# A hybrid S5 and dilated-attention layer: the turns of q and k stand apart, and V is two tiles

## The chip, the cores and the metric

The kernel runs on one core of a Trainium2 chip. A core has five engines, each with an instruction queue of its own that it works off in order: TensorE (PE; its weight loads are shown as PEld), VectorE (DVE), ScalarE (ACT), GpSimd (POOL) and SyncE (SP), which here mostly issues DMAs. [...] The metric is the time of one execution on the device in microseconds, the median of the runs.

## The reference

One decoder layer of width 1024 over 512 tokens, batch 1, everything in float32. A root-mean-square norm is followed by one wide projection, whose columns feed an S5 branch (a complex state-space scan with gates), an attention branch with a gate, and two merge gates. The branches are projected, gated, added, projected once more and added to the input. The attention branch is what the change touches:

```python
DILATED_GROUPS = ((128, 1), (512, 4), (2048, 16))
...
        h = rms_norm(x, norm_w[layer])
        proj = h @ w_in[layer].astype(f32)
        u_s, z_s, q, k, v, z_a, r_s, r_a = jnp.split(proj, offsets, axis=-1)
        y_s = s5_branch(u_s, ...)
        y_s = (y_s * jax.nn.silu(z_s)) @ w_ssm_out[layer].astype(f32)
...
        y_a = dilated_attention(q, k, v)      # q, k normed and rotated
        y_a = (y_a * jax.nn.silu(z_a)) @ w_attn_out[layer].astype(f32)
        m = jax.nn.sigmoid(r_s) * y_s + jax.nn.sigmoid(r_a) * y_a
        x = (x.astype(f32) + m @ w_o[layer].astype(f32)).astype(x.dtype)
...
        for g, (window, dil) in enumerate(DILATED_GROUPS):
            j = jnp.arange(window // dil + 1)
            idx = t[:, None] - dil * j[None, :]
            s = jnp.einsum('bqhd,bqjhd->bqhj', q_blk[:, :, g], kg) * scale
            lse = jax.nn.logsumexp(s, axis=-1)
            p = jnp.exp(s - lse[..., None])
            outs.append(jnp.einsum('bqhj,bqjhd->bqhd', p, vg))
            lses.append(lse)
        w = jax.nn.softmax(jnp.stack(lses), axis=0)
        return jnp.einsum('gbqh,gbqhd->bqhd', w, jnp.stack(outs))
```

Each of the 8 heads (64 wide) has three groups of q, k and v. Group 0 has dilation 1 and needs, for a block of 128 queries, its own block of keys and the one before it. Groups 1 and 2 are the dilated ones.

## The kernel before, in words

**Precision.** Every projection is done in three matmuls (`mm3`, L122): a number is split into a high part that TensorE can multiply at full speed and the rest, and hi·hi, hi·lo and lo·hi are added in PSUM. A weight tile arrives raw by DMA (`w_raw`, two buffers), ACT rounds it (`w_hi`, L108) and DVE or POOL subtracts (`w_lo`, L110); of these two there are three buffers each.

**Stages.** The program first does norm, S5 branch and gates; from about 440 us on it does the attention for four pairs of heads (loop `for hp in range(NP)`, L1094 to L1120), and then the last projections. In the loop for the pair `hp`:

- `scores(hp)`: products of queries and keys (tile `sps`), softmax on ACT, DVE and POOL. The result is `Pt`, the probabilities of both heads and both kinds: kind 0 is group 0, kind 1 the two dilated groups.
- `qk_first()`: a wide granule of projections (tile `pj`, four banks) that gives q and k of groups 0 and 1 for the next pair; norm on DVE, rotation on POOL (L852 to L857). The rotated results are the tiles `qraw`.
- `qk_second(hp + 1, mid)`: the granule that gives q and k of group 2 (`qraw`, copied by L903, their squares by L879 and L882) and V of groups 1 and 2 (copied by L905). It goes through the contraction in four steps `kq`, each with four rows of tokens `r`, and calls `mid` once per `kq`. `mid` puts in, between the projections: for kq = 1 the turn of group 0, for kq = 2 the turn of group 1, for kq = 3 the values of this pair.
- `v0_unit(hp + 1, V)`: the projection of V of group 0, then the turn of group 2, then `finv()`, which writes V of group 0 (L593).

A **turn** (`qk_turn`, L859) transposes q, and then k, of one group: four transposes into one PSUM bank (tile `qtp`, L67), from which ACT writes the high part (L873) and DVE the low part (L874). For k of groups 1 and 2 these are two halves of 64 partitions.

The **values** (`values`, L987) go in four pieces: kind 0 in two halves, then kind 1 in two halves. A piece transposes the probabilities of each head (four transposes into one bank, tile `ptp`; the first of kind 0 has three), ACT copies the bank of the first head to SBUF (`ptb`, L1027) and DVE that of the second (L1029); then TensorE multiplies with V (tile `ot`, L63, 30 products in all in one bank). The products of a piece stand behind the transposes of the next one. At the end DVE takes `ot` with its gate (L1036) and the result is split into `aT`.

**Banks.** `qtp`, `ptp`, `sps` and `vtp` share three banks (`ps_g`), `pj` has four (`ps_p`), and `ot` one (`ps_o`).

**V** is one tile for all three groups (`new_v`, L601, tag s6a, a single buffer). So every copy into it for the next pair waits for the last product that reads it for this one.

**What sets the order.** The code is written in the order above, but a scheduler of the framework orders the instructions of each engine by its own model of durations before the kernel is compiled. `with queued():` (L69) holds what stands under it behind the last matmul issued so far. On the chip an engine then works off its list in that order, and waits at each instruction for what it needs. In the names below, `pj<-hT_hi,w_hi` means output `pj` from inputs `hT_hi` and `w_hi`.

Of the kernel before, what the change touches and what calls it, by code (L numbers as in the profile page):

```python
# [11 lines left out]
F32 = mybir.dt.float32  # L12
# [8 lines left out]
P = 128  # L21
# [31 lines left out]
def tile_hybrid_block(ctx: ExitStack, tc: tile.TileContext, x, positions, norm_w, w_in, lam_re, lam_im,  # L53
# [529 lines left out]

    def v0_unit(hp, V):
        ps = cm_unit(hT_hi, hT_lo)
        vt = t2k("vt")
        act.copy(vt.rearrange("p (b r j) -> p r b j", r=4, b=4), ps.rearrange("p (r b j) -> p r b j", r=4, b=4))

        def finish():
            pt = bank("vtp")  # L590
            for b in range(NB):
                pe.transpose(pt[:, b * P:(b + 1) * P], vt[:, b * P:(b + 1) * P], ident)
            act.copy(V[:, 0].rearrange("p b c -> p (b c)"), pt)  # L593
        return finish

    def v_granule(hp, V):
        pss = tok_granule()
        for b in range(2):
            act.copy(V[:, 1:3, 2 * b:2 * b + 2], pss[b].rearrange("p (r g c) -> p g r c", r=2, g=2))

    def new_v():  # L601
        return big.tile([P, NG, NB, P], F32, name="V", tag="s6a")

# [213 lines left out]
    def wide_granule(th, tl, mid=None):  # L817

        pss = [ps_p.tile([P, 512], F32, name="pj", tag="pj") for _ in range(NB)]
        for kq in range(4):  # L820
            if mid:
                mid(kq)
            hi, lo = get_w()
            for r in range(NB):
                for k in range(2):
                    kk = 2 * kq + k
# [31 lines left out]

    def qk_turn(g, raw, QT, KA, KB):  # L859
        for a in range(2):  # L860
            ps = bank("qtp")
# [4 lines left out]
            if a == 0 or g == 0:  # L866
                parts = [(slice(0, P), QT[0][:, g], QT[1][:, g]) if a == 0 else (slice(0, P), KA[0], KA[1])]
            else:
                parts = [(slice(64 * h, 64 * h + 64), KB[0][64 * h:64 * h + 64, g - 1, h],
                          KB[1][64 * h:64 * h + 64, g - 1, h]) for h in range(2)]  # L870
            for sl, hi, lo in parts:
                w = wcol[sl, g, a:a + 1]
# [23 lines left out]
    def qk_second(hp, mid=None):  # L896
# [5 lines left out]
        for r in range(NB):  # L902
            act.copy(raw[:, r], pss[r][:, 0:256])  # L903
            squares(sq[:, r], pss[r][:, 0:256])
            act.copy(V[:, 1:3, r], pss[r][:, 256:512].rearrange("p (g c) -> p g c", g=2))  # L905
        qk_norm((2,), [raw], sq)
# [81 lines left out]
    def values(hp, Pt, V):  # L988
# [4 lines left out]
        def pv(kind, bb, pts):  # L993
            for i in range(2):
                b = 2 * bb + i
                for k in range(2):
                    if kind == 0 and b == 0 and k == 0:
                        continue
                    for h in range(2):
                        po = slice(64 * h, 64 * h + 64)  # L1000
                        if kind == 0:
                            v = V[:, 0, b - 1 + k, po]
                            o = ov[po, b]
                        else:
                            v = V[:, 1 + k, b, po]
                            o = ot[po, b * P:(b + 1) * P]
                        first = kind == 0 and b == 0
                        pe.matmul(o, v, pts[h][:, (2 * i + k) * P:(2 * i + k + 1) * P], start=first,
                                  stop=kind == 1 and b == NB - 1 and k == 1, skip_group_check=True)

        n = 0
        for kind in range(2):
            for bb in range(2):
# [80 lines left out]
    for hp in range(NP):  # L1094
        Pt = scores(hp, *QK)
        if hp < NP - 1:
            raws = qk_first()

            def mid(kq):
                if kq == 1:  # L1100
                    qk_turn(0, raws[0], *QK)
                if kq == 2:
                    with queued():
                        qk_turn(1, raws[1], *QK)
                if kq == 3:
                    values(hp, Pt, V)

            raw, V_next = qk_second(hp + 1, mid)
            V = V_next
            finv = v0_unit(hp + 1, V)  # L1110
            qk_turn(2, raw, *QK)
            finv()
        else:
# [3 lines left out]
            for c in range(n_ra + 1, KT - 2):  # L1117
                ra_unit(c)
            values(hp, Pt, V)
            for c in range(KT - 2, KT):  # L1120
# [61 lines left out]
```

## Time and profile before

| | |
|---|---|
| runs of the kernel before | 732.35, 732.63 and 736.42 us |
| median of them | 732.63 us |
| span of the profiled execution | 732.57 us |
| TensorE busy | 699.6 us (95%) |
| VectorE, ScalarE, GpSimd busy | 457.1, 314.6, 191.7 us |
| TensorE busy in the stretch of the four pairs (440 to 670 us) | 224.0 of 230.0 us |
| DMA, over the span | 82.14 MB, 112 GB/s |

A row of the timeline has the start in us from the span's start, the duration, engine, line and operation, output and inputs, the tile's size, how many instructions are put together in it, and in brackets the idle time of the engine before it with what it waited for. A matmul's row shows the time until its result is there, and the next one starts earlier than that, so the distance between the starts of two rows tells what a row takes on the engine.

### The profile page before, as it was taken

The page shows a single profiled execution, that of the slowest core. Times are in us where ns is not written, and L with a number is a line of the kernel's source. Part 1 is how long each engine was busy: PE and PEld are TensorE (multiplying, and loading weights), DVE is VectorE, ACT ScalarE, POOL GpSimd, SP SyncE. Part 2 cuts the span into 40 slices and gives each one's busy share as a digit, 9 for nine tenths or more (in the row PEclk, how much of TensorE's full clock was granted, in tenths as well). Part 3 has the DMA queues.
Part 4 walks back from the last instruction along what each step waited for, and adds up shares of the span by engine and source line. Part 5 has one row for each costly group of instructions (what it writes and reads, how often), then busy time and mean ns, then how long its engine had stood idle before and what let it go on. Part 6 is the DMA issues. An engine that isn't in the chain of part 4 may idle for free.

```text
span 732.6 us, 12680 instructions
## 1 busy us (share of the span) xinstructions
PE 699.6 (95%) x4821; PEld 574.2 (78%) x4821; DVE 457.1 (62%) x912; ACT 314.6 (43%) x631; POOL 191.7 (26%) x346
## 2 busy tenths in 40 slices
PE   2799899999999999999999999999989999999997
PEld 2687688778878787888888888788868877878886
DVE  6759673989946546764335659655664666464832
ACT  6434463332326465442144456537153734443420
POOL 3426540230205343550000316021601250230000
PEclk9999999999999999999999999999999999999999
DMA  8433653564547554455333432222412231326441
GB/s 203 106 96 94 171 144 77 137 149 132 120 131 153 122 103 133 139 168 172 99 100 87 130 87 79 66 58 58 115 31 79 65 89 30 115 73 236 139 144 57
DMA packets 137213, 82.14 MB, mean 112 GB/s; under 512 B 32696, under 2 KB 125632, under 8 KB 137024
## 3 DMA queue, kind: packets, MB, share of 16 engines
q1 hardware_dynamic: 135088, 78.96, 37.5%
q0 software_dynamic: 2048, 2.36, 2.6%
q8 instruction: 38, 0.62, 0.4%
q14 instruction: 23, 0.19, 0.1%
q10 hardware_dynamic: 16, 0.00, 0.0%
HBM read 68.46 MB, written 10.49 MB: 108 GB/s over the span
## 4 chain that ended last, share of the span: by engine, by line
PE 87%; DMA 4%; ACT 3%; DVE 3%; SPq 2%; issue 1%; ACTq 0%
PE pj L63 71%; DMA w_raw<-in_w_in_dram 3%; PE sps L63 3%; PE yps L63 3%; PE ot L63 2%; PE ptp L67 2%; PE kps L63 2%; PE xps L63 1%; PE qtp L67 1%; DMA Uj<-ud 1%; ACT w_hi L108 1%; SPq L442 1%; PE wps L67 1%; ACT qkp L873 1%; DVE w_lo L110 1%
## 5 line engine op out<-in xcount | busy, mean ns | idle before, releaser
L108 ACT ACTIVATE w_hi<-w_raw 128x1024 fp32r<-128x1024 f32 x100 | 106.0, 1061 | 236.8 <-PE pj L63 206.6
L110 DVE TENSOR_TENSOR w_lo<-w_raw,w_hi 128x1024 fp32r<-128x1024 f32 x98 | 124.3, 1268 | 107.9 <-ACT w_hi L108 107.2
L63 PE MATMUL pj<-hT_lo,w_hi 128*128 128x512 f32 (+1 forms) x344 | 132.9, 387 | 3.0 <-DVE hT_lo L251 3.0
L63 PE MATMUL pj<-hT_hi,w_hi 128*128 128x512 f32 (+1 forms) x344 | 132.8, 389 | 2.4 <-ACT V L905 1.4
L63 PE MATMUL pj<-hT_hi,w_lo 128*128 128x512 f32 (+1 forms) x344 | 132.4, 386 | 1.6 <-DVE w_lo L110 1.6
L63 PE MATMUL pj<-w_hi,hT_hi 128*128 128x512 f32 (+1 forms) x288 | 106.5, 372 | 0.0
L63 PE MATMUL pj<-w_lo,hT_hi 128*128 128x512 f32 (+1 forms) x288 | 106.5, 370 | 0.0
L63 PE MATMUL pj<-w_hi,hT_lo 128*128 128x512 f32 (+1 forms) x288 | 106.0, 371 | 0.0
L63 PEld LDWEIGHTS pj<-hT_lo,w_hi 128*128 128x128 f32 x344 | 66.0, 192 | 16.2 <-DVE hT_lo L251 3.9
L63 PEld LDWEIGHTS pj<-hT_hi,w_hi 128*128 128x128 f32 x344 | 65.5, 192 | 16.5 <-ACT V L905 2.1
L63 PEld LDWEIGHTS pj<-hT_hi,w_lo 128*128 128x128 f32 x344 | 65.9, 192 | 15.4 <-DVE w_lo L110 2.3
L63 PEld LDWEIGHTS pj<-w_hi,hT_hi 128*128 128x128 f32 x288 | 54.1, 188 | 10.0 <-issue 0.2
L63 PEld LDWEIGHTS pj<-w_hi,hT_lo 128*128 128x128 f32 x288 | 54.0, 188 | 10.0
L63 PEld LDWEIGHTS pj<-w_lo,hT_hi 128*128 128x128 f32 x288 | 54.0, 188 | 9.8
L931 ACT ACTIVATE Pt<-Pt,st 128x256 f32<-128x256 f32 (+1 forms) x64 | 31.0, 492 | 18.7 <-DVE st L929 18.7
L735 POOL TENSOR_TENSOR kt<-kt,dg 16x128 f32<-16x128 f32 x8 | 4.6, 571 | 125.0 <-ACT kt L734 118.4
L852 POOL TENSOR_TENSOR rt<-qraw,tC 128x256 f32<-128x256 f32 x12 | 14.3, 1189 | 87.7 <-DVE qraw L846 87.4
L739 POOL DMA_DIRECT2D dd<-kt x64 | 33.7, 535 | 2.4 <-POOL kt L735 2.4
L874 DVE SCALAR_TENSOR_TENSOR qkp<-qtp,wcol,qkp 128x512 fp32r<-128x512 f32 (+1 forms) x32 | 23.0, 745 | 13.5 <-ACT qkp L873 13.4
L961 POOL COPY sw<-st 32x4 f32<-32x4 f32 x64 | 12.0, 187 | 73.2 <-ACT Pt L931 70.5
L873 ACT ACTIVATE qkp<-qtp,wcol 128x512 fp32r<-128x512 f32 (+1 forms) x32 | 20.8, 685 | 15.7 <-PE qtp L67 10.4
L277 POOL TENSOR_TENSOR ab<-dd,AT 128x512 f32<-128x512 f32 x16 | 23.0, 1446 | 11.6 <-DVE ab L278 11.6
(263 smaller groups left out, 1289.4 us busy)
## 6 DMA issues: line engine op xcount, KB each, us to landing
w_raw<-in_w_in_dram SPq DMA_DIRECT2D x40, 512.0 KB
w_raw<-in_w_in_dram SPq DMA_DIRECT2D x112, 128.0 KB
w_raw<-in_w_glu_dram SPq DMA_DIRECT2D x8, 512.0 KB
w_raw<-in_w_ssm_out_dram SPq DMA_DIRECT2D x8, 512.0 KB
w_raw<-in_w_o_dram SPq DMA_DIRECT2D x8, 512.0 KB
x_all<-in_x_dram SPq DMA_DIRECT2D x4, 512.0 KB
ud<-uT SPq DMA_DIRECT2D x8, 256.0 KB
Uj<-ud SPq DMA_DIRECT2D x8, 256.0 KB
```

The costliest lines, as they stand in the source:

```text
L63: last[0] = nc.tensor.matmul(*a, **k)
L67: last[0] = nc.tensor.transpose(*a, **k)
L108: act.activation(hi, src, AF.Copy, scale=scale)
L110: e.tensor_tensor(lo, src, hi.bitcast(F32), op=ALU.subtract)
L277: eng.tensor_tensor(tv, a2.unsqueeze(2).broadcast_to(sh), ai, op=ALU.mult)
L442: sp.dma_start(D1[64 * h:64 * h + 64, a], bv[a][h])
L739: pool.dma_start(M[Q * t:Q * t + Q, :, 0:P - Q * t], kt[:, :, t:].rearrange("q g k p -> q g (k p)"))
L852: pool.tensor_tensor(t1, rh[:, :, :, 0:16], cv.broadcast_to([P, NB * 2, 2, 16]), op=ALU.mult)
L873: act.activation(hi, ps[sl], AF.Copy, scale=w)
L874: dve.scalar_tensor_tensor(lo, ps[sl], w, hi.bitcast(F32), op0=ALU.mult, op1=ALU.subtract)
L931: act.activation(o, o, AF.Exp, bias=nm, scale=-1.0, accum_out=st[:, kind, 1, h, b:b + 1])
L961: pool.tensor_copy(sw[32 * r:32 * r + 32, :, :, b], st[32 * b:32 * b + 32, 1, :, :, r])
```

## The change

- **V is two tiles.** `V0` (group 0, tag s6c) and `V` (groups 1 and 2, tag s6a). The copies L593 and L905 write to the one or the other.
- **The values come in two parts, the dilated groups first.** `values` is now a generator: kind 1, then a pause, then kind 0. The flags `start` and `stop` of the accumulation in `ot` are set accordingly. The first part is called from `mid` at (kq, r) = (3, 2), the second behind the whole granule, both held behind the last matmul. In the last loop both parts run one after the other.
- **A turn is put in by halves.** `qk_turn` takes the list of its parts (0 is q, 1 is k), and `mid` is called before each block of rows `r`: q of group 0 at (2, 1), k of group 0 at (2, 2), q of group 1 at (3, 0), k of group 1 at (3, 1), all held behind the last matmul.

```diff
@@ finish, v_granule, new_v
-            act.copy(V[:, 0].rearrange("p b c -> p (b c)"), pt)
+            act.copy(V[0].rearrange("p b c -> p (b c)"), pt)
...
-        return big.tile([P, NG, NB, P], F32, name="V", tag="s6a")
+        return (big.tile([P, NB, P], F32, name="V0", tag="s6c"), big.tile([P, 2, NB, P], F32, name="V", tag="s6a"))
@@ the granule that calls mid
         for kq in range(4):
-            if mid:
-                mid(kq)
             hi, lo = get_w()
             for r in range(NB):
+                if mid:
+                    mid(kq, r)
@@ qk_turn
-    def qk_turn(g, raw, QT, KA, KB):
-        for a in range(2):
+    def qk_turn(g, raw, QT, KA, KB, parts=(0, 1)):
+        for a in parts:
@@ qk_second
-            act.copy(V[:, 1:3, r], pss[r][:, 256:512].rearrange("p (g c) -> p g c", g=2))
+            act.copy(V[1][:, :, r], pss[r][:, 256:512].rearrange("p (g c) -> p g c", g=2))
@@ values
-                            v = V[:, 0, b - 1 + k, po]
+                            v = V[0][:, b - 1 + k, po]
...
-                            v = V[:, 1 + k, b, po]
+                            v = V[1][:, k, b, po]
...
-                        first = kind == 0 and b == 0
+                        first = kind == 1 and b == 0 and k == 0
...
-                                  stop=kind == 1 and b == NB - 1 and k == 1, skip_group_check=True)
+                                  stop=kind == 0 and b == NB - 1 and k == 1, skip_group_check=True)
...
-        for kind in range(2):
+        for kind in (1, 0):
+            if kind == 0:
+                yield
@@ the loop over the pairs
-            def mid(kq):
-                if kq == 1:
-                    qk_turn(0, raws[0], *QK)
-                if kq == 2:
+            done = values(hp, Pt, V)
+            steps = {(2, 1): (0, 0), (2, 2): (0, 1), (3, 0): (1, 0), (3, 1): (1, 1)}
+
+            def mid(kq, r):
+                if (kq, r) in steps:
+                    g, a = steps[kq, r]
                     with queued():
-                        qk_turn(1, raws[1], *QK)
-                if kq == 3:
-                    values(hp, Pt, V)
+                        qk_turn(g, raws[g], *QK, parts=(a,))
+                if (kq, r) == (3, 2):
+                    with queued():
+                        next(done)

             raw, V_next = qk_second(hp + 1, mid)
+            with queued():
+                next(done, None)
...
-            values(hp, Pt, V)
+            for _ in values(hp, Pt, V):
+                pass
```

What the scheduler makes of it is seen in the engines' lists. A row there is line, operation, output and inputs, shape, and the number of equal instructions in a row. The first 1747 rows of TensorE are the same in both kernels.

On TensorE in the second loop (hp = 1), from the end of the granule's projections on, the list of before is:

```order
L67 MATMUL qtp<-ident,qraw 128x4x32 x8
L67 MATMUL qtp<-ident,qraw 128x128 x8
L67 MATMUL ptp<-ident,Pt 128x128 x10
L63 MATMUL ot<-ptb,V 64x4x32
L67 MATMUL ptp<-ident,Pt 128x128 x4
L63 MATMUL ot<-ptb,V 64x4x32 x5
L67 MATMUL ptp<-ident,Pt 128x128 x4
L63 MATMUL ot<-ptb,V 64x4x32
L67 MATMUL ptp<-ident,Pt 128x128 x4
L63 MATMUL ot<-ptb,V 64x4x32 x7
L67 MATMUL ptp<-ident,Pt 128x128 x8
L63 MATMUL ot<-ptb,V 64x128 x16
```

And at the same place after the change (products of shape 64x128 are the dilated groups, 64x4x32 group 0):

```order
L67 MATMUL qtp<-ident,qraw 128x4x32 x8
L67 MATMUL qtp<-ident,qraw 128x128 x8
L67 MATMUL ptp<-ident,Pt 128x128 x12
L63 MATMUL ot<-ptb,V 64x128
L67 MATMUL ptp<-ident,Pt 128x128 x4
L63 MATMUL ot<-ptb,V 64x128 x7
L67 MATMUL ptp<-ident,Pt 128x128 x3
L63 MATMUL ot<-ptb,V 64x128
L67 MATMUL ptp<-ident,Pt 128x128 x3
L63 MATMUL ot<-ptb,V 64x128 x7
L67 MATMUL ptp<-ident,Pt 128x128 x8
```

The sixteen turns' transposes stay where they were. The dilated products come first; behind the last row shown stand six products of group 0, and the other eight follow between the next granule's projections, one behind 19 of them and seven behind three more. In the third loop the list is the same but for these eight, which stand together, and in before but for the two middle pieces, which stand as x8 and x8. In the first loop the four turns of after stand apart between projections, the products form seven runs (1, 7, 1, 7, 1, 5 and 8) where there were four (1, 5, 8 and 16); in the last loop there are four runs (8, 1, 7, 14) where there were three (6, 8, 16).

On ACT in the second loop, before, from the first turns' high parts (`qkp`) to the copies of V:

```order
L873 ACTIVATE qkp<-qtp,wcol 128x512 x2
L903 COPY qraw<-pj 128x256 x4
L873 ACTIVATE qkp<-qtp,wcol 128x512
L873 ACTIVATE qkp<-qtp,wcol 64x512
L1027 COPY ptb<-ptp 128x384
L873 ACTIVATE qkp<-qtp,wcol 64x512
L1027 COPY ptb<-ptp 128x512 x3
L879 ACTIVATE qsq<-pj 128x256
L905 COPY V<-pj 128x2x128
```

After (the copy of `ptb` is L1029 there):

```order
L903 COPY qraw<-pj 128x256
L879 ACTIVATE qsq<-pj 128x256
L903 COPY qraw<-pj 128x256
L873 ACTIVATE qkp<-qtp,wcol 128x512
L879 ACTIVATE qsq<-pj 128x256
L873 ACTIVATE qkp<-qtp,wcol 64x512
L1029 COPY ptb<-ptp 128x512
L873 ACTIVATE qkp<-qtp,wcol 64x512
L1029 COPY ptb<-ptp 128x512
L1029 COPY ptb<-ptp 128x384
L905 COPY V<-pj 128x2x128 x4
L1029 COPY ptb<-ptp 128x512
```

The first three rows are the end of an alternation of four copies L903 with three squares L879, which now stands ahead of the third L873; the copies of V stand ahead of the last copy of `ptb`.

On DVE at the same place, before:

```order
L874 SCALAR_TENSOR_TENSOR qkp<-qtp,wcol,qkp 128x512 x3
L874 SCALAR_TENSOR_TENSOR qkp<-qtp,wcol,qkp 64x512
L1029 COPY ptb<-ptp 128x384
L874 SCALAR_TENSOR_TENSOR qkp<-qtp,wcol,qkp 64x512
L1029 COPY ptb<-ptp 128x512 x3
L1036 SCALAR_TENSOR_TENSOR at<-ot,sza 128x512
L882 TENSOR_REDUCE ssq<-qsq 128x4 x4
L841 TENSOR_SCALAR qv<-ssq 128x16
```

And after (the copy of `ptb` is L1031):

```order
L874 SCALAR_TENSOR_TENSOR qkp<-qtp,wcol,qkp 128x512 x2
L882 TENSOR_REDUCE ssq<-qsq 128x4 x3
L874 SCALAR_TENSOR_TENSOR qkp<-qtp,wcol,qkp 128x512
L882 TENSOR_REDUCE ssq<-qsq 128x4
L874 SCALAR_TENSOR_TENSOR qkp<-qtp,wcol,qkp 64x512
L841 TENSOR_SCALAR qv<-ssq 128x16
L1031 COPY ptb<-ptp 128x512
L115 TENSOR_SCALAR qa<-qv 128x16
L874 SCALAR_TENSOR_TENSOR qkp<-qtp,wcol,qkp 64x512
L116 TENSOR_SCALAR qrstd<-qa 128x16
L1031 COPY ptb<-ptp 128x512
```

The reductions of the squares and the first steps of the norm behind them have moved from behind the values to between the turns' low parts.

More of the change, by code (lines that the diff above doesn't have):

```diff
@@ L598, in v_granule @@
         for b in range(2):
-            act.copy(V[:, 1:3, 2 * b:2 * b + 2], pss[b].rearrange("p (r g c) -> p g r c", r=2, g=2))
+            act.copy(V[1][:, :, 2 * b:2 * b + 2], pss[b].rearrange("p (r g c) -> p g r c", r=2, g=2))
     def new_v():
-        return big.tile([P, NG, NB, P], F32, name="V", tag="s6a")
+        return (big.tile([P, NB, P], F32, name="V0", tag="s6c"), big.tile([P, 2, NB, P], F32, name="V", tag="s6a"))
     scn = big.tile([P, 4096], F32, name="scn", tag="s3")
@@ L866, in qk_turn @@
             if a == 0 or g == 0:
-                parts = [(slice(0, P), QT[0][:, g], QT[1][:, g]) if a == 0 else (slice(0, P), KA[0], KA[1])]
+                ends = [(slice(0, P), QT[0][:, g], QT[1][:, g]) if a == 0 else (slice(0, P), KA[0], KA[1])]
             else:
-                parts = [(slice(64 * h, 64 * h + 64), KB[0][64 * h:64 * h + 64, g - 1, h],
+                ends = [(slice(64 * h, 64 * h + 64), KB[0][64 * h:64 * h + 64, g - 1, h],
                           KB[1][64 * h:64 * h + 64, g - 1, h]) for h in range(2)]
-            for sl, hi, lo in parts:
+            for sl, hi, lo in ends:
                 w = wcol[sl, g, a:a + 1]
```

## The prediction

> **What bounds the kernel now.** I read the page first: the busy shares, the granted clock, and the shares of the chain that ended last.
>
> ```profile
> span 732.6 us, 12680 instructions
> ...
> PE 699.6 (95%) x4821; PEld 574.2 (78%) x4821; DVE 457.1 (62%) x912; ACT 314.6 (43%) x631; POOL 191.7 (26%) x346
> ...
> PEclk9999999999999999999999999999999999999999
> ...
> PE 87%; DMA 4%; ACT 3%; DVE 3%; SPq 2%; issue 1%; ACTq 0%
> ```
>
> TensorE works for 95% of the span, and 87% of the chain is its own work. So the kernel can only gain where TensorE idles, and it loses whenever the order gives TensorE more to do or to wait for. The second view is TensorE's waits, summed over the stretch from 440 to 670 us, which is where the four head pairs run and the change acts.
>
> ```profile
> PE qtp L67 <- DVE qkp L874: 3.5, 2, 1.8
> PE pj L63 <- ACT V L905: 1.4, 3, 0.5
> PE ptp L67 <- DVE qkp L874: 1.0, 2, 0.5
> ```
>
> The columns are the total, the number of waits and the longest one. The wait for V, which splitting V can remove, is 1.4 us over three loops, 0.47 us in each. The turns (qtp waiting for a PSUM bank) cost 3.5 us in two waits, and the first transposes of the probabilities 1.0 us in two. Together this is 5.9 us. One per cent of the run, about what a measurement of this kernel can tell from no change, is 7.3 us. So even a change that removed all three would not be a clear gain.
>
> The third view is the timeline of TensorE in the second loop (hp = 1), from the first turn to the first projection after the values. An ot product leaves two records, so x14 there is seven instructions.
>
> ```profile
> 530.68 1.47 PE L67 MATMUL qtp<-ident,qraw 128*128 128x128 f32 x12
> 533.91 0.66 PE L67 MATMUL qtp<-ident,qraw 128*128 128x128 f32 x4 [1.76 <-DVE qkp L874]
> 534.57 0.55 PE L67 MATMUL ptp<-ident,Pt 128*128 128x128 f32 x3
> 535.60 0.98 PE L67 MATMUL ptp<-ident,Pt 128*128 128x128 f32 x7 [0.48 <-DVE qkp L874]
> 536.51 0.43 PE L63 MATMUL ot<-ptb,V 128*64 128x128 f32 x2
> 536.88 0.65 PE L67 MATMUL ptp<-ident,Pt 128*128 128x128 f32 x4
> 537.46 0.87 PE L63 MATMUL ot<-ptb,V 128*64 128x128 f32 x10
> 538.26 0.66 PE L67 MATMUL ptp<-ident,Pt 128*128 128x128 f32 x4
> 538.85 0.43 PE L63 MATMUL ot<-ptb,V 128*64 128x128 f32 x2
> 539.21 0.66 PE L67 MATMUL ptp<-ident,Pt 128*128 128x128 f32 x4
> 539.80 1.09 PE L63 MATMUL ot<-ptb,V 128*64 128x128 f32 x14
> 540.81 1.09 PE L67 MATMUL ptp<-ident,Pt 128*128 128x128 f32 x8
> 541.84 1.97 PE L63 MATMUL ot<-ptb,V 128*64 128x128 f32 x32
> 544.28 0.50 PE L63 MATMUL pj<-hT_hi,w_hi 128*128 128x512 f32 x1 [0.47 <-ACT V L905]
> ```
>
> From 530.68 to 544.28 this island takes 13.60 us. There are three banks for transposes: the fourth turn waits for the bank of the first, and the second group of ptp for that of the third turn. What empties these banks is ACT (hi part) and then DVE (lo part):
>
> ```profile
> 531.84 1.25 ACT L873 ACTIVATE qkp<-qtp,wcol 128x512 fp32r<-128x512 f32 x2
> 532.98 1.19 ACT L903 COPY qraw<-pj 128x256 f32<-128x256 f32 x4
> 534.02 1.27 ACT L873 ACTIVATE qkp<-qtp,wcol 128x512 fp32r<-128x512 f32 x2
> ...
> 544.12 0.39 ACT L879 ACTIVATE qsq<-pj 128x256 f32<-128x256 f32 x1
> 544.39 0.38 ACT L905 COPY V<-pj 128x256 f32<-128x256 f32 x1
> ```
>
> ```profile
> 531.97 1.22 DVE L110 TENSOR_TENSOR w_lo<-w_raw,w_hi 128x1024 fp32r<-128x1024 f32 x1 [4.32 <-ACT w_hi L108]
> 533.11 1.40 DVE L874 SCALAR_TENSOR_TENSOR qkp<-qtp,wcol,qkp 128x512 fp32r<-128x512 f32 x2
> 534.79 1.40 DVE L874 SCALAR_TENSOR_TENSOR qkp<-qtp,wcol,qkp 128x512 fp32r<-128x512 f32 x2 [0.28 <-ACT qkp L873]
> 536.18 0.56 DVE L1029 COPY ptb<-ptp 128x384 f32<-128x384 f32 x1
> ...
> 537.73 0.69 DVE L1029 COPY ptb<-ptp 128x512 f32<-128x512 f32 x1
> ...
> 544.46 1.61 DVE L882 TENSOR_REDUCE ssq<-qsq 128x4 f32<-128x256 f32 x4
> 546.10 0.17 DVE L841 TENSOR_SCALAR qv<-ssq 128x16 f32<-128x16 f32 x1
> ```
>
> DVE is only 62% busy over the span, but here its queue sets TensorE's start: the first L874 ends at 533.11 + 0.70 = 533.81 and the turn goes on at 533.91.
>
> **The change part by part.** No arithmetic is added or removed. Counts and shapes of transposes and products stay, as do DMAs, so no DMA queue (SP's included) and no POOL work is moved past anything. The two V tiles are copied with the same eight copies. What changes is order.
>
> *The V wait.* The copies L905 then wait only for the products of the dilated groups, which stand in the middle of the island. ACT has them behind it before the projection needs the banks, so 0.47 us goes in each of three loops: −1.4 us, the bound of the gain being the whole row.
>
> *The turns.* They are asked for at four points between projections. In the first loop the order does spread them. In loops two and three it does not: all sixteen qtp still stand in one row behind the last projection of the granule, as before. The cause I see is POOL, which still rotates the raw q and k then:
>
> ```profile
> 526.51 1.73 POOL L857 TENSOR_TENSOR qraw<-rt,rt 128x256 f32<-128x256 f32 x1
> ...
> 529.98 0.74 POOL L857 TENSOR_TENSOR qraw<-rt,rt 128x256 f32<-128x256 f32 x1
> ```
>
> The rotations end at 528.24 and 530.72, and the island begins at 530.68. So the 1.76 us waits of loops two and three stay: 0.
>
> *The queue behind the turns in loops two and three.* Counting from the first qtp, the waits now stand behind other work. On ACT, the four squares L879 go between the copies L903. Seven of these eight now stand ahead of the third L873 at a pitch of 0.26 us (544.12 to 544.39): they run from 2.30 to 4.16, where before the L873 began at 3.34. On DVE three of the reductions L882 (1.61/4 = 0.40 us each) come between the second and the third L874. The two L874 end at 3.83, the reductions at 4.97, the third L874 (0.70 us) at about 5.71, and ptp group two starts at 5.78 instead of 535.60 − 530.68 = 4.92: +0.86 us. Group four needs the bank that DVE's first copy of ptp empties, and that copy now stands behind the fourth reduction (0.40), a 64-row L874 (0.70) and L841 (0.2): it ends at about 7.61, so group four starts at 7.68. Each of these durations is a row of the trace. Their starts assume that DVE runs them back to back. If the reductions found their squares later, the wait would be longer.
>
> *The pieces.* From 7.68 I list the order of after with start-to-start times of the rows above: ptp x4 0.59 (538.26 to 538.85), ot x7 1.01 (539.80 to 540.81), ptp x3 0.48 (0.59 less one transpose of 0.11), ot x1 0.36, ptp x3 0.48, ot x7 1.01, ptp x8 1.03, ot x6 0.91 (0.80 of five and one more). That is 5.87, the projection starts at 13.55. The eight products left, one and seven, stand later between projections: 0.36 + 1.01 = 1.37. The island is worth 14.92 instead of 13.60 us: **+1.3 us** in loop two, and I take the same for loop three, whose waits in the summed view come in the same pairs (3.5 us in two, 1.0 us in two). One run of transposes followed by one of products costs 1.03 − 8 x 0.11 + 1.01 − 7 x 0.11 = about 0.4 us beyond its instructions, at 0.11 us for a transpose, (1.09 − 0.66)/4, and for a product, (0.87 − 0.43)/4. Such runs rise from five to seven in loop two, and from four to six in loop three.
>
> *Loop one.* There the turns already stood clear of the values, and no bank wait is listed. Runs rise from four to seven: 3 x 0.40 − 0.47 = **+0.7 us**. *The last loop* has three runs by the order and gets four: **+0.4 us**. Its dilated probabilities are scaled last, by DVE, but before they are needed; bounds 0 and +0.8, a run's price less or more.
>
> Sum: 1.3 + 1.3 + 0.7 + 0.4 = +3.7 us. The profiled span of 732.6 stands 0.03 us under the median of the runs, so **736.3 us**. The bounds: only the V wait goes and nothing else costs, 732.6 − 1.4 = 731.2, and with both ptp waits gone too 730.2; at the upper end the clock below and a second bank wait in each loop, about 742. I take the list, since each of its rows is in the trace.
>
> **The clock, a rival that speaks against the change.** The same island in the third loop is longer, though its order is almost the same:
>
> ```profile
> core 0: us, PE busy (x) PEld busy (x) DVE busy (x) ACT busy (x) POOL busy (x), PEclk, DMA share, GB/s
> 530.68:544.28 13.60, 10.88 (x108) 8.40 (x106) 7.75 (x11) 7.93 (x17) 0.04 (x1) 1.00 0.16 45
> 601.09:615.58 14.49, 11.77 (x107) 9.24 (x106) 7.76 (x11) 7.92 (x17) 0.04 (x1) 0.88 0.13 38
> 606.00:609.00 3.00, 2.99 (x12) 2.33 (x13) 1.92 (x3) 1.33 (x3) 0.00 (x0) 0.50 0.24 72
> ```
>
> 14.49 − 13.60 = 0.89 us, with a granted clock of 0.50 from 606 to 609. From the first turn to the first product pass 536.51 − 530.68 = 5.83 us in loop two, with the clock at 1.00. After the change the same stretch is 5.78 + 0.87 + 0.2 = 6.9 us, and it is thinner. If that brings the half clock into loop two as well, and for a longer time into loop three, the price is 0.9 us each: 736.3 + 0.9 to 1.8 = 737.2 to 738.1, and with loop one too 739.0.
>
> [...]
>
> **The other rivals.** *Gain only*: the V wait goes, and DVE's queue turns out not to be in the way, because the squares reach it late enough for the L874 to pass or because the runs' price is hidden under the copies. The time is 730.2 to 731.5, faster than before, though by under 1%. It decides if the second ptp group starts no later than 4.9 us after the first qtp. For it speaks that TensorE waits only 0.48 us there now; against it, that the order on DVE is fixed and has three reductions in front. *It does not do what it says*: in loops two and three the turns stay in one row, as the order shows. If the later waits cost only what the V wait gives back, the time is 732 to 735. *Something else is late*: the scores of the next head pair or the last loop's scaling becomes a wait of over 2 us; nothing in the rows shows it. 740 and more.
>
> **How the numbers follow.** The list 735 to 737.5: 0.46. Little net, 732 to 735: 0.22. Half clock, 737.5 to 740: 0.12. Gain only, under 732: 0.12. Unseen, over 740: 0.08. The range 732.0 to 740.0 holds the first three, 0.80. Faster by over 1% (under 725.3) would need more than all listed waits: 0.02. Slower by over 1% (over 740.0): 0.08. Same: 0.90.
>
> **What would show it.** In the waits of TensorE, pj on V L905 should be gone in all three loops; if it stays, the V step is wrong. qtp on L874 should still cost 1.8 us twice. ptp on L874 should rise from 0.48 to about 1.3 in loops two and three, and a new wait of ptp on DVE's ptb copy of about 0.5 should appear; if it doesn't, the queue step is wrong and the time is nearer 734. Islands: 14.9 us from first qtp to the last product, projections between taken off. The granted clock there decides the clock rival. Turns that do stand spread in the trace of loops two and three, or a total under 731, would overturn the forecast.

## The result and the profile after

The changed kernel took 740.38 us in the median of six runs (738.79 to 743.70); the kernel before, six runs beside it, 735.1 us (732.35 to 736.68). The ratio is 1.0075, with a 95% interval from 1.0049 to 1.0100. The change makes the kernel slower by 3.6 to 7.4 us. The forecast was 736.3 us, with a range that ended at 740.0: the direction was right, and the time lies just outside.

The profile page of the changed kernel:

```profile
span 738.4 us, 12669 instructions
...
PE 704.5 (95%) x4821; PEld 576.1 (78%) x4821; DVE 454.8 (62%) x912; ACT 314.2 (43%) x631; POOL 188.1 (25%) x346
...
PEclk9989899999999999999999999999999999999999
```

TensorE has 4.9 us more of busy time (704.5 against 699.6) for the same 4821 matmuls, 1.1 us of it ahead of the four loops. So most of the loss is not listed as waiting; and the granted clock is lower in two slices at the start. The waits of TensorE after, in the stretch from 430 to 680 us:

```profile
PE qtp L67 <- DVE qkp L874: 3.5, 2, 1.8
PE ptp L67 <- DVE qkp L874: 2.4, 2, 1.2
PE ptp L67 <- DVE ptb L1031: 0.5, 2, 0.4
```

The wait for V is gone (1.4 us), the two waits of the turns stand where they stood, the wait of ptp has grown from 1.0 to 2.4 us, and one on DVE's copy is new. Net, the waits grew by 0.5 us only. The second loop after, from the first turn to the next granule:

```profile
532.83 1.47 PE L67 MATMUL qtp<-ident,qraw 128*128 128x128 f32 x12
536.06 0.66 PE L67 MATMUL qtp<-ident,qraw 128*128 128x128 f32 x4 [1.76 <-DVE qkp L874]
536.72 0.66 PE L67 MATMUL ptp<-ident,Pt 128*128 128x128 f32 x4
538.58 1.12 PE L67 MATMUL ptp<-ident,Pt 128*128 128x128 f32 x8 [1.20 <-DVE qkp L874]
539.63 0.43 PE L63 MATMUL ot<-ptb,V 128*64 128x128 f32 x2
540.23 0.66 PE L67 MATMUL ptp<-ident,Pt 128*128 128x128 f32 x4 [0.17 <-DVE ptb L1031]
540.82 1.09 PE L63 MATMUL ot<-ptb,V 128*64 128x128 f32 x14
...
545.19 0.88 PE L63 MATMUL ot<-ptb,V 128*64 128x128 f32 x12
546.00 0.50 PE L63 MATMUL pj<-hT_hi,w_hi 128*128 128x512 f32 x1
```

Group two of ptp starts 538.58 − 532.83 = 5.75 us after the first turn (4.92 before). DVE's rows say why: three reductions stand between the second and the third L874.

```profile
535.26 1.41 DVE L874 SCALAR_TENSOR_TENSOR qkp<-qtp,wcol,qkp 128x512 fp32r<-128x512 f32 x2
536.58 1.06 DVE L882 TENSOR_REDUCE ssq<-qsq 128x4 f32<-128x256 f32 x3
537.77 0.75 DVE L874 SCALAR_TENSOR_TENSOR qkp<-qtp,wcol,qkp 128x512 fp32r<-128x512 f32 x1
538.44 0.41 DVE L882 TENSOR_REDUCE ssq<-qsq 128x4 f32<-128x256 f32 x1
```

To see where the time went, I divide the span at the same instructions in both kernels: the first turn of loops one, two and three, the first projection behind the island of loop three (the turns and values in one piece, as in the second loop), and the first projection behind the last values. The columns are the stretch, its length, each engine's busy time with its instructions, then the granted clock, DMA share and GB/s. After:

```profile
0.00:455.61 455.61, 432.25 (x3330) 357.21 (x3331) 297.28 (x530) 198.69 (x374) 136.41 (x202) 0.99 0.47 125
455.61:532.83 77.22, 77.08 (x422) 61.76 (x421) 48.75 (x131) 35.32 (x82) 21.84 (x61) 1.00 0.25 73
532.83:604.63 71.80, 68.67 (x384) 54.54 (x382) 41.81 (x113) 33.41 (x81) 17.49 (x45) 1.00 0.23 67
604.63:618.18 13.55, 10.21 (x92) 7.70 (x90) 11.48 (x27) 9.40 (x22) 1.15 (x3) 1.00 0.18 51
618.18:672.95 54.77, 54.77 (x330) 44.35 (x329) 24.05 (x70) 22.58 (x54) 9.92 (x35) 1.00 0.25 77
672.95:738.40 65.45, 61.49 (x271) 50.59 (x270) 31.41 (x42) 14.76 (x18) 1.29 (x1) 0.99 0.43 149
```

And before:

```profile
0.00:454.26 454.26, 431.18 (x3331) 355.81 (x3331) 298.04 (x530) 198.59 (x374) 137.06 (x203) 0.99 0.48 125
454.26:530.68 76.42, 75.86 (x423) 61.52 (x421) 48.62 (x131) 35.34 (x82) 22.50 (x61) 1.00 0.27 76
530.68:601.09 70.41, 67.69 (x383) 54.58 (x382) 42.48 (x113) 33.50 (x81) 18.67 (x46) 1.00 0.24 69
601.09:615.58 14.49, 11.77 (x107) 9.24 (x106) 7.76 (x11) 7.92 (x17) 0.04 (x1) 0.88 0.13 38
615.58:667.13 51.55, 51.55 (x312) 42.44 (x312) 28.89 (x87) 24.50 (x60) 12.12 (x37) 1.00 0.26 82
667.13:732.60 65.47, 61.50 (x272) 50.60 (x270) 31.30 (x42) 14.76 (x18) 1.28 (x1) 1.00 0.43 149
```

The last stretch is equal. The four loops take 217.34 us instead of 212.87, which is 4.47 us more, and the stretch ahead of them, in which nothing was changed, 1.35 us more. One number hides a clock: before had 0.88 granted in the island of loop three, after 1.00 everywhere in the loops.

### The profile page after: what moved, and what is told of

It reads as the page before. It is cut to its first block, busy times and chain, and to the rows that moved or that the text cites. A ratio compares the mean times of both kernels' runs of the same rounds, so it can differ in the third digit from the quotient of the medians.

```text
span 738.4 us, 12669 instructions
## 1 busy us (share of the span) xinstructions
PE 704.5 (95%) x4821; PEld 576.1 (78%) x4821; DVE 454.8 (62%) x912; ACT 314.2 (43%) x631; POOL 188.1 (25%) x346
## 4 chain that ended last, share of the span: by engine, by line
PE 87%; DVE 4%; DMA 3%; ACT 3%; SPq 2%; issue 1%; ACTq 0%
PE pj L63 71%; PE sps L63 3%; PE yps L63 3%; PE ot L63 2%; DMA w_raw<-in_w_in_dram 2%; PE kps L63 2%; PE ptp L67 2%; PE xps L63 1%; DMA Uj<-ud 1%; PE qtp L67 1%; SPq L442 1%; PE wps L67 1%; DVE w_lo L110 1%; ACT w_hi L108 1%; ACT qkp L873 1%
## 5 line engine op out<-in xcount | busy, mean ns | idle before, releaser
L874 DVE SCALAR_TENSOR_TENSOR qkp<-qtp,wcol,qkp 128x512 fp32r<-128x512 f32 (+1 forms) x32 | 23.3, 745 | 9.1 <-ACT qkp L873 8.6
L873 ACT ACTIVATE qkp<-qtp,wcol 128x512 fp32r<-128x512 f32 (+1 forms) x32 | 21.3, 689 | 15.3 <-PE qtp L67 9.4
L978 POOL COPY sfb<-sd 32x2 f32<-32x2 f32 x64 | 18.0, 282 | 34.0 <-DVE sd L974 31.3
```

The costliest lines, as they stand in the source:

```text
L873: act.activation(hi, ps[sl], AF.Copy, scale=w)
L874: dve.scalar_tensor_tensor(lo, ps[sl], w, hi.bitcast(F32), op0=ALU.mult, op1=ALU.subtract)
L978: pool.tensor_copy(fb[32 * b:32 * b + 32, :, r], d[32 * r:32 * r + 32, 1, :, b])
```

## The experiments

All are compared by the attention stretch, from the first turn of loop one to the first projection behind the last values, and by the ratio of their runs to runs of the kernel before on the same chip.

**V in two tiles, nothing else.** Based on the change, with calls and order of before:

```diff
-        for kind in (1, 0):
-            if kind == 0:
+        for kind in (0, 1):
+            if kind == 1:
                 yield
...
+            def mid(kq, r):
+                if r:
+                    return
+                if kq == 1:
+                    qk_turn(0, raws[0], *QK)
+                if kq == 2:
+                    with queued():
+                        qk_turn(1, raws[1], *QK)
+                if kq == 3:
+                    for _ in values(hp, Pt, V):
+                        pass
```

> V as two tiles and nothing else: values in the old order (group 0 first), turns as before. The attention stretch, from the first turn in the loop of the first head pair (454.26 us in the profile of before) to the first projection behind the last values (667.13), takes 212.87 us before and 217.34 us after the change. Theory (what is gained hangs on the dilated products being early, not on the tiles): the copies L905 still wait for the last products, the wait of pj on V stays at 0.47 us three times, stretch 212.9 us, ratio 1.000. Rival (the second tile alone frees the copies): wait gone, 211.5 us, ratio 0.998.

Ratio 1.0012 (0.9993 to 1.0030): no change that can be told. The wait on V stays, as the theory had it:

```profile
PE pj L63 <- ACT V L905: 1.4, 3, 0.5
```

Yet the stretch was 211.45 us, not 212.9. The two loops ahead of it are those of before to 0.01 us, so the tiles gave nothing; the difference is the island of loop three:

```profile
600.92:614.01 13.09, 10.37 (x108) 8.24 (x106) 7.75 (x11) 7.92 (x17) 0.04 (x1) 1.00 0.14 42
614.01:665.55 51.54, 51.54 (x312) 42.50 (x313) 28.89 (x87) 24.50 (x60) 12.11 (x37) 1.00 0.26 82
```

The same list took 14.49 us at a granted clock of 0.88 and 13.09 us at 1.00. So 1.40 us of the kernel before is a spell of half clock (0.50 from 606 to 609 us), and this profile is the kernel before at full clock: 211.45 us. Against that, the change costs 217.34 − 211.45 = 5.9 us.

**The dilated groups first, in one piece.** As the run above, with `for kind in (1, 0)`.

> Two tiles and the dilated groups first, but the values in one piece and the turns as before. By the order, runs of products stay at 4, 5, 4 and 3 in the four loops, and the sums of squares (L882) stay behind the values on DVE. Theory (the loss comes from the reductions ahead of the turns and from more runs): the wait on V goes, nothing else comes, stretch 212.87 - 1.4 = 211.5 us, ratio 0.998. Rival (dilated first costs by itself, since its first group has four transposes and another bank order): stretch 213.5 us or more, with a wait of ptp.

Ratio 0.9993 (0.9976 to 1.0010), not to be told from 1. No wait on V was left. The first two loops took 75.77 and 70.02 us instead of 76.42 and 70.41, a gain of 0.65 and 0.39. The stretch was 211.93 us with the same granted clock in loop three as before (0.97; 212.87 us): a gain of 0.94, less than 1.4, as loop three and the last one gave none. The rival is wrong: dilated first costs nothing in the first two loops. This run also settles what lengthened the wait of `ptp` in the changed kernel. The turns stand in one row in loop two here too, but DVE's reductions come behind the values (from 544.53 us, the first turn at 530.62), and the wait is not 2.4 us but

```profile
PE ptp L67 <- DVE qkp L874: 0.7, 2, 0.4
```

**Values in parts, turns as before.** The change with `mid` calling the turns as in the kernel before:

```diff
             def mid(kq, r):
-                if (kq, r) in steps:
-                    g, a = steps[kq, r]
+                if kq == 1 and r == 0:
+                    qk_turn(0, raws[0], *QK)
+                if kq == 2 and r == 0:
                     with queued():
-                        qk_turn(g, raws[g], *QK, parts=(a,))
+                        qk_turn(1, raws[1], *QK)
```

> The change without the halves of the turns: turns as before, values in two parts, two V tiles. The lists of TensorE in loops two, three and four are those of the changed kernel; in loop one the products form five runs instead of seven. Theory (the parts carry the loss, the turns almost none): ptp waits 2.4 us on L874 and 0.5 us on ptb, stretch 217.34 - 2 x 0.4 = 216.5 us, ratio 1.005. Rival (the halves of the turns carry it): 213.5 us or less, ratio 1.001 or less.

Ratio 1.0107 (1.0078 to 1.0137): the parts carry the loss. The stretch of this profile was 219.42 us, with granted clocks of 0.95 and 0.97 in the second and third loop, and in the second island:

```profile
532.09:547.50 15.41, 12.46 (x92) 9.41 (x90) 10.83 (x27) 9.39 (x22) 0.00 (x0) 0.78 0.17 46
```

A second profile of it, taken later for this, was expected thus:

> Values in parts, turns as before, a second time. Theory: at full clock the attention stretch is 217.3 - 0.8 = 216.5 us; the first profile had 219.4 us with granted clocks of 0.95 and 0.97 in loops two and three, so it lies between, by the spells; ahead of it 454 to 456 us. Rival (the longer islands always bring half clock here): 219 us again.

Its clock was 1.00 in the loops and its stretch 216.19 us, with loops one and two at 76.26 and 71.78 us. So the lower clock comes or stays away with the same list, and at full clock the parts cost 4.7 us of the 5.9.

**Turns in halves, values whole.** Two tiles, old order of the groups, `mid` with the change's table of steps:

> Two V tiles, the turns in halves as in the change, the values in one piece in the old order. TensorE's lists of loops two, three and four are those of the kernel before; in loop one the products form six runs instead of four. Theory: loop one +0.8 us, nothing else, the wait of pj on V (1.4 us) stays; stretch 212.2 us at full clock, ratio 1.001. Rival (the halves take over a gain in loop one, as the turns are hidden there): stretch 211.0 us or less.

Ratio 1.0021 (1.0001 to 1.0042). Loop one took 77.41 us, 1.0 more than at full clock before; the waits of before stayed. Loops two to four have TensorE's list of before and took 139.5 us instead of 135.0, at granted clocks of 0.98 and 0.94 in loops two and three, so the stretch of 216.92 us is no measure of the turns. That of loop one is.

**More runs, nothing else.** The products of a piece in two halves, each behind the transposes of one bank (a tile of 128 x 512 floats in PSUM, which TensorE writes and ACT or DVE copies out); on the run with two tiles:

```diff
                     pts.append(pt)
-                pend.append((kind, bb, pts))
-                if len(pend) > 1:
-                    pv(*pend.pop(0))
+                    if pend:
+                        with queued():
+                            pv(*pend[0], half=(h,))
+                if pend:
+                    pend.pop(0)
+                pend.append((kind, bb, pts))
```

> The kernel with two V tiles in the old order, only that the products of a piece are issued in two halves, each behind the transposes of one bank. By the order, runs of products rise from 4, 5, 4 and 3 to 7, 6, 6 and 6 (nine more), no list of ACT or DVE has other work. Theory (each pair of a run of transposes and one of products costs 0.4 us, whatever waits): stretch 211.45 + 9 x 0.4 = 215.1 us at full clock, ratio 1.005. Rival (pieces are free; what the changed kernel lost was only waits): 211.5 to 212.3 us, ratio 1.000 to 1.001.

Ratio 1.0033 (1.0016 to 1.0050). The stretch was 215.79 us at full clock:

```profile
454.77:532.35 77.58, 76.87 (x423) 61.72 (x421) 48.69 (x131) 35.24 (x82) 22.49 (x61) 1.00 0.26 74
532.35:603.33 70.98, 68.27 (x384) 54.71 (x382) 42.47 (x113) 33.49 (x81) 18.67 (x46) 1.00 0.24 68
603.33:670.56 67.23, 64.52 (x420) 51.48 (x418) 36.63 (x97) 32.43 (x76) 12.17 (x38) 1.00 0.24 71
```

Against 76.41, 70.41 and 64.63 us that is 1.17 for three runs, 0.57 for one, and 2.60 for five: 4.34 us for nine, 0.48 us each, with only one new wait of 0.2 us. Pieces are not free.

The records, taken singly, divide this price in two. A product leaves two records. In a long run those of two products start 0.007 us apart and the next two 0.10 us behind them, so two products take the time of one; a product alone takes its two records one after the other. In the run with two tiles the 240 records of the four loops begin at 128 separate starts, here at 144: the halving leaves products without a partner. At 0.103 us from one start to the next, sixteen starts are 1.7 us. The other 2.6 us are the changes, 0.29 us for each of the nine: the last transpose and the last product of a run take 0.20 us to the next start instead of 0.11, the first of each 0.16 instead of 0.11.

The longer distances stand where the form of the rows changes: transposes are 128\*128, products with V 128\*64. Turns between projections (both 128\*128) show no such gap: in the traces of before and after alike, a projection ahead of a turn takes 0.23 us to the next start, as one ahead of its like, and the last transpose of a turn and the projection behind it take 0.34 us together (0.03 and 0.31), as much as 0.11 and 0.23. Among the scores, in the run with two tiles, the last one of 128\*128 ahead of one of 64\*128 takes 0.209 us to the next start, one ahead of its like 0.119. No run here took the form away, so that it is the form was not shown.

**The squares late.** The change, with the third group's squares and norm behind the values:

```diff
         for r in range(NB):
             act.copy(raw[:, r], pss[r][:, 0:256])
-            squares(sq[:, r], pss[r][:, 0:256])
             act.copy(V[1][:, :, r], pss[r][:, 256:512].rearrange("p (g c) -> p g c", g=2))
-        qk_norm((2,), [raw], sq)
-        return raw, V
+
+        def norm():
+            for r in range(NB):
+                squares(sq[:, r], raw[:, r])
+            qk_norm((2,), [raw], sq)
+        return raw, V, norm
...
             with queued():
                 next(done, None)
+            norm()
```

> The changed kernel, but the squares of the third group (L879, L882) and its norm are issued behind the second part of the values, and read q and k from SBUF instead of PSUM. By the order this also lets the turns of loops two and three stand apart. Theory (what cost was DVE's queue between the turns): no wait of qtp or ptp on L874 is left (3.5 and 2.4 us) and none of ptp on ptb, stretch 217.34 - 6.4 = 210.9 us, ratio 0.997. Rival (the cost is the pieces, the more often TensorE changes between turns, transposes and products, the more it loses): stretch over 214 us. Second rival (q and k of the third group are late and TensorE waits for them at their turn): qtp on qraw appears as a wait of 1 us or more per loop.

Ratio 0.9990 (0.9971 to 1.0009), against 1.0075 of the change: this one edit takes the loss away, though it does several things at once: the reductions leave DVE's queue, the turns of loops two and three stand apart, the products there stand in five runs in each loop instead of seven and six, and the scores of the last pair stand in five runs again. The stretch was 211.58 us, and the waits in it:

```profile
PE ptp L67 <- DVE Pt L988: 2.4, 3, 1.7
PE qtp L67 <- POOL qraw L857: 0.9, 2, 0.5
```

No wait on L874 is left. In its place ptp waits, in the last loop above all, for the probabilities of the dilated groups, which DVE scales last. The expectation of 210.9 did not count that.

**Two faster versions.** The first takes the run with the dilated groups in one piece, the late squares, and in the last loop group 0 first:

> Two V tiles and dilated groups first in the loops, turns and values called as in the kernel before, the third group's squares and norm issued behind the values (as in the run with late squares), and in the last loop group 0 first again. Theory: the run with late squares stood at 211.6 us for the attention stretch, of which 2.4 us were ptp waiting for the probabilities of the dilated groups, scaled last, nearly all in the last loop; group 0 first there takes 2 us of it away, and the first loop has two runs of products fewer (0.8 us). Stretch 208.8 us, against 211.45 us that the kernel before takes with the clock at 1.00 (the run with two tiles shows that); ratio 0.996. Rival (the turn of the third group, now late, and the changed order eat the gain): stretch 210.5 us or more, ratio 0.999 to 1.001.

Ratio 0.9937 (0.9918 to 0.9956): faster than before and after. Its stretch was 211.1 us, more than expected, through the last loop: TensorE waited 1.78 us for DVE's copy of ptb behind the scaling, and the granted clock fell behind it, to 0.77 from 658 to 661 us and 0.66 from 661 to 664.

```profile
658.28 0.87 PE L63 MATMUL ot<-ptb,V 128*64 128x128 f32 x10 [1.78 <-DVE ptb L1034]
...
661.57 1.79 PE L67 MATMUL ptp<-ident,Pt 128*128 128x128 f32 x8
```

The eight transposes at 661.57 took 1.79 us instead of 1.09. The stretch is only 1.8 us shorter than that of before (212.9), while the medians lie 4.9 us apart (731.1 against 736.0). The six runs have mean granted clocks of 0.992 to 0.994, the 23 runs of before 0.986 to 0.995, so a part of the ratio goes with a higher granted clock; whether the order brings that is not shown. The second version moves one gate unit ahead of the values in the last loop:

```diff
-            for c in range(n_ra + 1, KT - 2):
+            for c in range(n_ra + 1, KT - 1):
                 ra_unit(c)
...
-            for c in range(KT - 2, KT):
+            for c in range(KT - 1, KT):
                 ra_unit(c)
```

> The fastest kernel so far with one change: in the last loop one more gate unit is issued ahead of the values instead of behind them. There TensorE waited 1.78 us for DVE's copy of ptb, which stands behind the scaling of the probabilities, and 0.28 us for that scaling, and the granted clock was 0.77 and 0.66 for six us behind it. From the first turn to the end it took 211.11 + 65.41 = 276.5 us. Theory (nine more projections, 2.1 us, now stand ahead of the values and cover the wait): 276.5 - 2.1 = 274.4 us, and 272.8 us if the clock stays at 1.00; ratio 0.991. Rival (the scaling comes later by as much, or the end now waits for the last split): 276 us or more, ratio 0.994.

Ratio 0.9926 (0.9900 to 0.9952), 728.89 us in the median. From the first turn to the end it took 209.53 + 63.40 = 272.93 us (278.34 in the first profile of before), and the wait on ptb is down to 0.2 us:

```profile
454.17:663.70 209.53, 208.37 (x1232) 168.96 (x1230) 132.81 (x341) 102.11 (x239) 52.38 (x143) 1.00 0.26 75
663.70:727.10 63.40, 59.46 (x263) 48.85 (x261) 31.39 (x42) 14.58 (x18) 1.28 (x1) 0.98 0.42 150
```

**The stretch ahead of the change.** In the first profiles it took 1.35 us longer in the changed kernel, though the lists there are the same. Three runs were for that:

> The changed kernel once more, beside the others on one chip. Theory: the attention stretch is 217.3 us at full clock in every profile, and the stretch ahead of it (455.6 us in the first profile, 454.1 to 455.8 in the others) differs by the granted clock and the first DMAs alone: ratio 1.008. Rival (the stretch ahead of the first changed instruction is longer through the change): it is 455.5 us or more again, while the other kernels of this call stay below 455.

> The kernel before once more, for its clock. Theory: the attention stretch is 211.45 us plus 1.4 us for a spell of half clock in the third loop where there is one; the stretch ahead of it is 454 to 456 us, by the spells of half clock between 30 and 100 us (0.94 and 0.96 granted in the first profile). Rival (the kernel before always has one spell less there than the changed one): 454.5 us or less.

> The changed kernel a third time. Theory: attention stretch 217.3 us; ahead of it 454 to 456 us, at a granted clock between 30 and 60 us of 0.89 or 0.94 as it falls. Rival (the changed kernels always have 0.89 there, as in all three profiles so far): 455.5 us or more.

The changed kernel took 455.92 us there in the second profile and 453.77 in the third; the kernel before 455.11. The ratio of the repeated change was 1.0070 (1.0048 to 1.0092). The second profile alone spoke for the rival, the third does not. Between 30 and 60 us the granted clock was 0.94 in the first profile of before and 0.89 in the second; of the changed kernel's three, 0.89, 0.89 and 0.94. So it falls either way in both. The loops, in contrast, repeat: 217.34, 217.30 and 217.32 us after, 212.87 and 212.89 before, with a granted clock of 0.97 from the island of loop three to the last values both times.

## Why the prediction was right or wrong, point by point

- **The wait for V** goes: as forecast, and the runs show what does it: with two tiles alone it stays, with the dilated products early as well it is gone.
- **The turns** stay in a row in loops two and three, 3.5 us: as forecast. The reason given, POOL's rotations, fits the rows (the last one after ends at 532.50, the island begins at 532.83), but it is not the whole of it: with late squares the turns of these loops stand apart, with 0.9 us of waiting for the rotations.
- **The queue on DVE**: group two at 5.75 us (forecast 5.78), group four at 7.40 (forecast 7.68). DVE's rows show the reductions in between, and with late squares no wait on L874 is left; there the turns also stand apart, so that run does not tell the two apart. The run with the dilated groups in one piece does: turns in a row, reductions behind, and the wait of `ptp` at 0.7 us. One sum is off by a little: 3.83 + 3 x 0.40 is 5.03, not 4.97, for the end of the reductions; they ended at 4.81.
- **Loops two and three**: at full clock before took 70.41 us in loop two, after 71.80: +1.39 for the +1.3 forecast. That is partly luck. The island ended after 13.17 us, not 13.55, and the eight products behind it took the forecast 1.37 (1.38); but the 216 projections of the rest of the loop took 51.37 us from start to start instead of 50.86, +0.5, for which the sum had no term. In loop three the island takes 13.55 us plus 1.02 for the eight products put behind (623.82 − 622.80, below), 14.57 against 13.09: +1.48.
- **Loop one**: 77.22 − 76.41 = +0.81, for +0.7.
- **The last loop** is the term that was mis-sized: +0.4 forecast. From the island of loop three to the end of the values the full-clock run has 51.54 us; after has 54.77 less those 1.02, so **+2.2**. I had counted runs of products with V only. But the earlier norm of the third group also let the scheduler bring its turn, and with it the scores of the next pair, forward, and in the last loop this divided the scores into seven runs instead of five, and those of 64 rows by heads. In the trace after:

```profile
622.80 1.09 PE L63 MATMUL ot<-ptb,V 128*64 128x128 f32 x16
623.82 0.50 PE L63 MATMUL pj<-hT_lo,w_hi 128*128 128x512 f32 x1
...
639.24 1.76 PE L63 MATMUL sps<-qkp 128*128 128x256 f32 x12
640.93 0.50 PE L63 MATMUL pj<-hT_lo,w_hi 128*128 128x512 f32 x1
...
641.59 0.95 PE L63 MATMUL sps<-qkp 64*128 64x128 f32 x6
642.47 0.50 PE L63 MATMUL pj<-hT_hi,w_hi 128*128 128x512 f32 x1
...
645.46 1.20 PE L63 MATMUL sps<-qkp 64*128 64x256 f32 x12
```

  and in the run with two tiles, where the last thirty stand in two runs, of eighteen and twelve:

```profile
641.10 1.76 PE L63 MATMUL sps<-qkp 128*128 128x256 f32 x18
642.79 0.50 PE L63 MATMUL pj<-hT_hi,w_lo 128*128 128x512 f32 x1
...
646.85 0.40 PE L63 MATMUL pj<-hT_lo,w_hi 128*128 128x512 f32 x1
647.17 0.99 PE L63 MATMUL sps<-qkp 64*128 64x256 f32 x12
648.10 0.50 PE L63 MATMUL pj<-hT_hi,w_lo 128*128 128x512 f32 x1
648.43 0.39 PE L63 MATMUL pj<-hT_hi,w_hi 128*128 128x512 f32 x1
```

  A row has the form of its first instruction: the eighteen are six scores of 128 rows and twelve of 64, the x12 at 639.24 is six and six, and the x6 at 641.59 the other six of 64. So the same eighteen took 642.79 − 641.10 = 1.69 us there, and 1.69 + 0.88 = 2.57 after. Taken singly, the twelve of 64 rows start in six pairs there, the two of a pair 0.003 to 0.004 us apart; by the code, a pair is one score of each head. After, the six of one head stand in one run and the six of the other in the next, and each starts alone, 0.11 to 0.17 us behind the one before it. This loss of partners is +0.88 us; the last run of twelve lost 0.2 the same way.

  A projection, 512 columns of split numbers, takes 0.23 us from start to start (0.46 ns a column; a transpose of 128 columns of float32 takes 0.11 us, 0.85 ns a column). The one ahead of a piece of 64 rows takes 647.17 − 646.85 = 0.32, and the one behind it 648.43 − 648.10 = 0.33: 0.2 us for going in and out. Added up from start to start, the 48 scores of the last pair took 4.74 us there and 5.83 after, +1.1; the same 162 projections 38.34 and 38.90, +0.6; the thirty products 3.73 and 4.28, +0.55. So the step that failed is the +0.4 of the last loop: it priced one more run of products, and put the scores and the projections beside the pieces at nothing. The order of the changed kernel showed the division, and the prediction said of the scores only that nothing spoke for a wait.
- **The sum** at full clock: 0.81 + 1.39 + 1.48 + 2.20 = 5.88 us, for 3.7. Between the profiles stand 5.8: the lost 5.88, less the 1.40 of half clock that before had in loop three and after had not, plus the 1.35 ahead of the loops.
- **The level.** The prediction set the span of 732.6 beside the median of 732.63 and took the 0.03 between them for the distance of span and time. In the runs with both, a time is 1.8 us above its span (740.17 and 738.4), and three runs were few: six gave 735.1. With its own +3.7 on 735.1 the forecast is 738.8; with the measured +5.9, 741.0. This base and the last loop together put the time outside the range; either alone would have left it inside (732.6 + 5.9 = 738.5, and 735.1 + 5.9 − 1.8 = 739.2).
- **The clock rival** did not come about: half clock was expected to strike the longer islands, and it struck loop three of the kernel before (two profiles of two) and none of the three profiles after; the kernel with parts had a lower clock (0.95 and 0.97 in loops two and three) in one profile of two. A spell cost 1.0 to 3.0 us in a loop where it came (55.00 against 54.03 us in loop three of the kernel with parts, 59.74 against 56.77 in that of the turns in halves), not 0.9: the prediction took 14.49 − 13.60, against loop two, while the island of loop three itself takes 13.09 at full clock. That a longer or thinner island brings it on was the author's supposition; no run shows it.
- **The other rivals.** *Gain only* hung on group two of `ptp` starting no later than 4.9 us; it started at 5.75. *It does not do what it says* had the turns right, and the later waits cost more than the V wait gave back. The time lies in the band of *something else is late*, over 740 us, but not by its mechanism: no wait of over 2 us came, the scores lost their time as work of TensorE.

## What to carry to other kernels

TensorE, busy 95% of the time here, paid for the change of order in pieces (0.48 us for each of nine further pairs of runs by the run with more runs, 1.1 us for the divided scores of the last pair) as well as in waits (0.5 us more): count how often the engine changes between forms of work in the whole list, also where the change only reaches through the scheduler, and look whether small products that start in pairs still stand beside their partners. Before work is put nearer to its consumer, look at who empties the buffers there; here a reduction that nobody waited for had slipped in front of the operation that everybody waited for, and issuing it later took the stretch from 217.34 to 211.58 us, more than the change itself was after (1.4 us). Take the base from times, not from spans, and from more than three runs where 1% matters.

## What was not expected of the hardware

- The same list at the same place took 13.09 or 14.49 us, by whether the granted clock fell to 0.50 for some 3 us; another 13.17 and 15.41 us, at a mean clock of 1.00 and 0.78. Runs of the kernel before on one chip spread from 731.6 to 737.3 us (29 runs). The time goes with the mean granted clock of a run: the twelve runs of before at 0.995, of all those beside the experiments, took 731.5 to 733.8 us, the six at 0.986 took 736.6 to 737.4. The stretch behind the loops was the same to 0.1 us wherever the same work stood in it. What sets off a spell was not found.
- Nine more pairs of a run of transposes (128\*128) and a run of products (128\*64) cost 0.48 us of TensorE's time each, nearly all of it shown as busy time (4.2 of 4.34 us): 0.29 us for the changes, and the rest for products that no longer had a partner to start with.
- Products with V (64 columns), of two heads, start 0.007 us apart when they stand side by side, and scores of 64 rows 0.003 to 0.021 us; a list that sets one head's behind the other's loses that: eighteen scores took 1.69 us in one order and 2.57 us in another.
